# Moving part of a background computation from the first product of a channel mixer to the second one

## The chip, the cores and the metric

The kernel runs on one NeuronCore of a Trainium2 chip. The metric is the device time of one execution in microseconds, as the median of several runs. All work is float32 in and out.

## The reference

Two layers act on a sequence of 1024 tokens with 1024 features. Each layer has a token mixer (layer 0: attention with forget gates, layer 1: gated linear attention) and a channel mixer. Each of the two stands behind an RMS norm whose result is scaled and shifted, and its output is multiplied by a gate. Shift, scale and gate come from a conditioning vector `c`:

```
c_act = jax.nn.silu(c)
mod = c_act @ ada_w[i] + ada_b[i]                  # 6 x 1024 per layer
sh1, sc1, g1, sh2, sc2, g2 = jnp.split(mod, 6)
x = x + g1 * mixer_i(modulate(rms_norm(x, norm1_g[i]), sh1, sc1))
h = modulate(rms_norm(x, norm2_g[i]), sh2, sc2)
x = x + g2 * ((silu(h @ gate) * (h @ up)) @ ffn_w_out[i])   # hidden size 2816
```

The six vectors of a layer do not depend on `x`, so the kernel computes them one at a time beside other work. The second layer's vectors are numbered from 0 here; the "second modulation vector" is `sc1` of layer 1 (the pair `(1, 1)` in the code). It is first needed when layer 1 norms its input, right after the channel mixer of layer 0.

## The kernel before

**Products.** Every float32 operand is split into a rounded part `hi` and a rest `lo`, and `mm3` (lines 317, 318, 319) issues three matmuls for each 128x128 block of weights: hi by hi, hi by lo, lo by hi. ScalarE makes `hi` (line 175), VectorE the rest (line 176). Line 319 is the one that needs the `lo` of the weights. The same lines 175 and 176 serve every such split.

**The channel mixer** is the function `ffn`. Its first product (`h @ ffn_w_in`) goes through 22 groups, a gate group and an up group for each of 11 pairs of hidden tiles. Two groups are computed plainly (`plain_tile`); the other 20 stand in the loop `for X in gs[2:]`. Each of these does seven block products in place of eight, by sums of operands. One block product is a call of `prod`, with 4 blocks, so 12 matmuls into one PSUM bank. VectorE adds the banks up (line 1745), ScalarE and GpSimd form the gated hidden tiles (lines 1728, 1730), GpSimd forms sums of them (lines 1703 to 1713), and they are stored to DRAM (line 1675). GpSimd also forms the sums of weights (lines 978 to 996).

The second product (`... @ ffn_w_out`) runs over three chunks of the hidden tiles, with 3, 4 and 4 tile pairs. Chunks 0 and 1 are the loop `for c_ in range(OC - 1)`: four blocks `i`, each with seven calls of `prod`, of 9 matmuls in chunk 0 and 12 in chunk 1. VectorE adds the results onto tiles `x` and `z` (line 1956). At the end of each block of chunk 1, GpSimd combines them (lines 1970 to 1974), and VectorE adds the gated result to the residual (line 1977), which was loaded from `x_sp` (line 1889). In the last of the four blocks the additions of line 1977 are put off. The third chunk accumulates in PSUM banks `f0a`, `f0b` and so on, and line 2005 adds them. Its operands `B11o`, `T1o`, `T2o`, `B22o` are fetched by line 1860 during chunk 1, and those named `ex_s` there are raw and are split on chip into `T3o` (line 1622 on ScalarE, line 1623 on VectorE). The third chunk's first group reads `B11o`, then `T1o`, then `T2o`.

**The modulation vectors** run beside this. `Pace` is a queue of generators with a balance: each call adds its argument to the balance, and as long as the balance is not negative the next step of a generator is emitted and its price is taken off. `prod` calls two such queues. `ada1` (line 1739) does gate 2 of layer 0 and vector 0 of layer 1 into `ad_s` (lines 541, 543). `ada1l` (line 1740) does the second vector of layer 1 with `ada_one`: it loads 256 KB of `ada_w` in four DMAs into the single buffer `far` (line 454), and two VectorE operations (line 497 for the very first, line 499 otherwise) multiply it and add it to `near`, 16 times over. One such round of a load and two operations is called a step here. Its price is 2.0: 0.5 behind the operations and 1.5 behind the next load. The next load overwrites `far`, so it waits on the two operations. After the 16th step the generator yields 500.0, so its closing product (`ada_end`, line 460, four small matmuls on `near`) is made only by the flush behind chunk 1.

**What sets the order.** The kernel gives no hand-written order for these engines. A scheduler of the tile framework places each engine's instructions, from the order in which they are emitted, their dependencies and its own estimates; `tc.issue_after(last_of("D"))` makes each operation of line 499 come behind the VectorE instruction emitted last before it. Each engine then works in its fixed order, and so does the SyncE queue that issues all these DMAs: an instruction that waits holds what stands behind it.

Of the kernel before, what the change touches and what calls it, by code (L numbers as in the profile page):

```python
# [53 lines left out]
def trunk(ctx, tc, x, c, ada_w, ada_b, norm1_g, norm2_g, ffn_w_in, ffn_w_out,  # L54
# [513 lines left out]
            while self.q:  # L568
                self(1.0)

    late_rate = [0.03]
    ada0, ada0p, ada1, ada1l = Pace(), Pace(), Pace(), Pace()

    def ada1_queue(js, acc, raws_):
# [1004 lines left out]
    def ffn(l, oh, xs, slots, nm, mid, norm_end, each=None, blocks=None):  # L1579
# [142 lines left out]
        def dest(G, key):  # L1722
            return tmpv[TMP[key]] if G.kind else gate_view(G.i, key)

        def fin(G, key):
            d = gate_view(G.i, key)
            if G.kind == 0:
                nc.scalar.activation(d, d, AF.Silu)
                return
            nc.gpsimd.tensor_mul(d, d, dest(G, key))  # L1730
            hid_done(G.i, key)

        def prod(w, t):
            ps = pin([P, HALF], F32, f"p{l}")
            n = len(t)
            for k in range(n):
                mm3(ps, w.hi[:, k, :], w.lo[:, k, :], hi(t[k]), lo(t[k]), k == 0, k == n - 1)
            tick()
            ada1(0.64 * n)
            ada1l(late_rate[0] * n)  # L1740
            return ps

        def add(G, key, ps, src=None):
            d = dest(G, key)
            nc.vector.tensor_add(d, d if src is None else dest(G, src), ps)  # L1745
# [101 lines left out]
        def part(c_):  # L1847

            raw_ = late_raw if c_ else early_raw
            n_k = ODS[c_]  # L1850
            nms = ONAMES if c_ < OC - 1 else ENAMES
            order = list(range(7 * n_k)) if c_ else list(FIRST)
            tiles, ys = o[c_], {}
            for nm_ in ONAMES:
                tiles[nm_] = [None] * n_k
            at = lambda n: (nms[n // n_k], n % n_k)

            def fetch(dst, src):
                with tc.issue_after(pre[0]) if pre else ExitStack():
                    nc.sync.dma_start(dst, src)  # L1860
                if c_ == OC - 1:
                    pre[:] = [last_of("S")]

            def load_raw(n):
                nm_, k = at(n)
                if is_raw(nm_, OAT[c_] + k) and n not in ys:
                    ys[n] = raw_()
                    fetch(ys[n], hid_d[(nm_, OAT[c_] + k)])

            pre = []  # L1870
            for j, n in enumerate(order):
                nm_, k = at(n)
                t = tiles[nm_][k] = big.tile([P, 2, HALF], FR, tag=SL[c_][n], name=f"{nm_}o{l}{c_}{k}")
                load_raw(n)
                if n in ys:
                    split_t(t, ys[n])
                else:
                    fetch(t.bitcast(F32), hid_d[(nm_, OAT[c_] + k)])
                for ahead in order[j + 1:j + 4]:
                    load_raw(ahead)  # L1880
                yield
# [11 lines left out]
        def advance(n):  # L1893
            while n_nxt[0] < n:
                next(nxt[0], None)
                n_nxt[0] += 1

        for X in gs[2:]:
            up = lambda n: advance(n) if X is gs[-1] else None
            if X is gs[-2]:  # L1900
                ada1.flush()
                late_rate[0] = 0.12
                nxt[0] = part(0)
                advance(4)
            nc.scalar.copy(dest(X, C11), prod(feed.next(), B11))
            p5 = prod(feed.next(), T1)
            up(8)
            add(X, C12, prod(feed.next(), T2), C11)
            up(11)
            add(X, C11, prod(feed.next(), B21))  # L1910
            fin(X, C11)
            add(X, C22, prod(feed.next(), T3), C12)
            add(X, C12, p5)
            up(15)
            add(X, C21, prod(feed.next(), T4), C22)
            fin(X, C21)
            add(X, C22, p5)
            fin(X, C22)
            up(20)
            add(X, C12, prod(feed.next(), B22))  # L1920
            fin(X, C12)
            up(21)
# [163 lines left out]

    ADA_A, ADA_B = 6.0, 3.0
    ffn(0, oh, xs, slots, "fo", lambda: mid(5, 6), norm_mixer)
    h1 = hs1
    after_norm = marks.pop("G0")  # L2090
# [525 lines left out]

    ADA_A, ADA_B = 12.0, 6.0
    ffn(1, None, xs, slots, "go", lambda: mid(11), final_norm, final_scale, (out_blocks, out_ends))
    dump("xb1", xs)

# [28 lines left out]
```

## Time and profile before

| | |
|---|---|
| median of 3 runs | 2345.26 us (2344.12 to 2349.59) |
| the profiled execution's own time | 2345.56 us |
| its span, first to last instruction | 2343.8 us |
| busy: TensorE / VectorE / ScalarE / GpSimd | 2322.6 / 1772.7 / 1128.0 / 1160.5 us |
| mean granted clock of TensorE | 0.997 |
| moved by DMA | 390.72 MB |

Times inside the profile are microseconds from the start of the span. The loop of the first product with its 20 groups lies at about 683 to 1068, chunk 0 of the second product at 1068 to 1125, chunk 1 at 1125 to 1201, and the third chunk starts at 1201.7. Layer 1 follows. In the views, PE is TensorE, DVE is VectorE, ACT is ScalarE, POOL is GpSimd and SP is SyncE, whose queue issues the DMAs. A bracket behind an instruction gives the idle time of its engine before it and what ended it. The profile models the ends of matmuls, so PE's busy time overstates how well it is used; the starts of matmuls show its pace.

### The profile page before, as it was taken

The page shows a single profiled execution, that of the slowest core. Times are in us where ns is not written, and L with a number is a line of the kernel's source. Part 1 is how long each engine was busy: PE and PEld are TensorE (multiplying, and loading weights), DVE is VectorE, ACT ScalarE, POOL GpSimd, SP SyncE. Part 2 cuts the span into 40 slices and gives each one's busy share as a digit, 9 for nine tenths or more (in the row PEclk, how much of TensorE's full clock was granted, in tenths as well). Part 3 has the DMA queues.
Part 4 walks back from the last instruction along what each step waited for, and adds up shares of the span by engine and source line. Part 5 has one row for each costly group of instructions (what it writes and reads, how often), then busy time and mean ns, then how long its engine had stood idle before and what let it go on. Part 6 is the DMA issues. An engine that isn't in the chain of part 4 may idle for free.

```text
span 2343.8 us, 35552 instructions
## 1 busy us (share of the span) xinstructions
PE 2322.6 (99%) x12088; PEld 1980.6 (85%) x12088; DVE 1772.7 (76%) x2946; ACT 1128.0 (48%) x2166; POOL 1160.5 (50%) x1027
## 2 busy tenths in 40 slices
PE   8999999999999999999999999999999999999999
PEld 7988888888888888788888899898888888888888
DVE  6577677776788888997888666668787777876787
ACT  6566566675544333334325654345444333345236
POOL 1345454533446656665563522345456666664651
PEclk9999999999999999999999999999999999999999
DMA  8533343352435545459774443555434544458674
GB/s 259 163 99 112 109 120 107 113 169 84 153 100 175 187 158 176 154 203 315 267 265 155 136 128 99 151 171 172 150 102 162 174 147 159 141 189 300 237 264 141
DMA packets 359342, 390.72 MB, mean 167 GB/s; under 512 B 26908, under 2 KB 296376, under 8 KB 359160
## 3 DMA queue, kind: packets, MB, share of 16 engines
q1 hardware_dynamic: 359160, 388.45, 50.7%
q8 instruction: 95, 1.56, 0.3%
q14 instruction: 87, 0.71, 0.1%
HBM read 287.10 MB, written 101.25 MB: 166 GB/s over the span
## 4 chain that ended last, share of the span: by engine, by line
PE 54%; DVE 4%; DMA 3%; POOL 2%; issue 2%; SPq 0%; ACT 0%; POOLq 0%; DVEq 0%; ACTq 0%
PE p_b L317 11%; PE p_b L319 11%; PE p_b L318 11%; PE gv_b L317 1%; PE gv_b L319 1%; PE gv_b L318 1%; PE gr_b L317 1%; PE gr_b L319 1%; PE gr_b L318 1%; DVE o_s L176 1%; DVE ad_s L543 1%; DMA ex_s<-x_sp 1%; PE gqp_b L317 0%; PE gk_b L317 0%; PE f1a_b L319 0%
## 5 line engine op out<-in xcount | busy, mean ns | idle before, releaser
L175 ACT CAST o_s<-xv_s 128x512 fp32r<-128x512 f32 (+1 forms) x392 | 235.9, 610 | 328.4 <-PE p_b L319 218.5
L176 DVE TENSOR_TENSOR o_s<-xv_s,o_s 128x512 fp32r<-128x512 f32 (+1 forms) x392 | 332.7, 854 | 37.2 <-ACT o_s L175 36.3
L317 PE MATMUL p_b<-B,o_s 128*128 128x512 f32 x608 | 235.4, 391 | 0.9 <-DVE ex_s L1745 0.5
L318 PE MATMUL p_b<-B,o_s 128*128 128x512 f32 x608 | 236.1, 389 | 0.0
L319 PE MATMUL p_b<-B,o_s 128*128 128x512 f32 x608 | 235.1, 389 | 0.0
L978 POOL TENSOR_TENSOR ex_s<-xv_s,xv_s 128x512 f32<-128x512 f32 (+1 forms) x64 | 96.0, 1499 | 238.8 <-DMA xv_s<-in_ffn_w_in_dram 123.3
L1362 POOL TENSOR_SCALAR lp_s<-lp_s,st 128x128 f32<-128x128 f32 (+7 forms) x128 | 98.9, 775 | 220.9 <-DVE st L1361 191.8
L317 PE MATMUL p_b<-T,o_s 128*128 128x512 f32 x480 | 186.7, 390 | 1.8 <-DVE x L1745 1.8
L318 PE MATMUL p_b<-T,o_s 128*128 128x512 f32 x480 | 186.7, 389 | 0.0
L319 PE MATMUL p_b<-T,o_s 128*128 128x512 f32 x480 | 181.2, 389 | 0.0
L1360 ACT ACTIVATE lp_s<-lp_s,st 128x128 f32<-128x128 f32 (+7 forms) x128 | 99.5, 777 | 85.4 <-DVE st L1356 68.1
L317 PEld LDWEIGHTS p_b<-B,o_s 128*128 128x128 f32 x608 | 114.1, 188 | 26.6 <-issue 1.6
L319 PEld LDWEIGHTS p_b<-B,o_s 128*128 128x128 f32 x608 | 114.1, 188 | 23.9
L318 PEld LDWEIGHTS p_b<-B,o_s 128*128 128x128 f32 x608 | 114.2, 188 | 23.2
L980 POOL TENSOR_TENSOR xv_s<-ex_s,xv_s 128x512 f32<-128x512 f32 (+1 forms) x64 | 95.7, 1495 | 51.2 <-DVE o_s L176 47.9
L1745 DVE TENSOR_TENSOR ex_s<-ex_s,p_b 128x512 f32<-128x512 f32 x140 | 94.2, 680 | 29.9 <-PE p_b L319 29.6
L990 POOL TENSOR_TENSOR xv_s<-xv_s,xv_s 128x512 f32<-128x512 f32 x48 | 65.8, 1370 | 97.9 <-issue 54.7
L176 DVE TENSOR_TENSOR pt_s<-t_b,pt_s 128x512 fp32r<-128x512 f32 (+1 forms) x160 | 98.4, 632 | 20.3 <-ACT pt_s L175 19.1
L317 PEld LDWEIGHTS p_b<-T,o_s 128*128 128x128 f32 x480 | 90.1, 188 | 21.3 <-DVE x L1745 2.2
L175 ACT CAST pt_s<-t_b 128x512 fp32r<-128x512 f32 (+1 forms) x160 | 82.6, 544 | 51.1 <-PE t_b L1382 32.6
L319 PEld LDWEIGHTS p_b<-T,o_s 128*128 128x128 f32 x480 | 90.1, 188 | 18.7
L318 PEld LDWEIGHTS p_b<-T,o_s 128*128 128x128 f32 x480 | 90.1, 188 | 18.6
(1539 smaller groups left out, 7378.2 us busy)
## 6 DMA issues: line engine op xcount, KB each, us to landing
xv_s<-in_ffn_w_in_dram SPq DMA_DIRECT2D x176, 256.0 KB, 3.2
hid_B<-x SPq DMA_DIRECT2D x66, 512.0 KB, 3.0
ad_s<-in_ada_w_dram SPq DMA_DIRECT2D x384, 64.0 KB, 2.4
hid_T<-x SPq DMA_DIRECT2D x44, 512.0 KB, 2.9
xv_s<-in_ffn_w_out_dram SPq DMA_DIRECT2D x88, 256.0 KB, 3.6
T2o<-hid_T SPq DMA_DIRECT2D x22, 512.0 KB, 7.0
T1o<-hid_T SPq DMA_DIRECT2D x22, 512.0 KB, 6.2
B11o<-hid_B SPq DMA_DIRECT2D x22, 512.0 KB, 5.9
```

The source lines that it names most:

```text
L175: nc.scalar.copy(hi, src)
L176: nc.vector.tensor_sub(lo, src, hi.bitcast(F32))
L317: nc.tensor.matmul(ps, ah, bh, start=start, stop=False, skip_group_check=chain)
L318: nc.tensor.matmul(ps, ah, bl, start=False, stop=False, skip_group_check=chain)
L319: nc.tensor.matmul(ps, al, bh, start=False, stop=stop, skip_group_check=chain)
L543: nc.vector.scalar_tensor_tensor(acc, raw[:, t], c42[:, o:o + 1], acc, op0=ALU.mult, op1=ALU.add)
L978: nc.gpsimd.tensor_add(s1, a21, a22)
L980: nc.gpsimd.tensor_sub(a11, s1, a11)
L990: nc.gpsimd.tensor_sub(r[A12], r[A12], r[A11])
L1360: nc.scalar.activation(lp, lp, AF.Exp, bias=mcur, scale=-1.0, accum_out=st[:, qi, 2:3])
L1362: nc.gpsimd.tensor_scalar(lp, lp, st[:, qi, 3:4], 1.0, op0=ALU.mult, op1=ALU.mult)
L1745: nc.vector.tensor_add(d, d if src is None else dest(G, src), ps)
```

## The change

Two numbers change, no line is added.

```
@@ -568,7 +568,7 @@
-    late_rate = [0.03]
+    late_rate = [0.0]
...
@@ -1899,7 +1899,7 @@
             if X is gs[-2]:
                 ada1.flush()
-                late_rate[0] = 0.12
+                late_rate[0] = 0.17
```

`late_rate` is what line 1740 adds to the balance of `ada1l` for each block of a product. Before, the first 18 groups of the loop (126 calls with 4 blocks) add 126 x 4 x 0.03 = 15.1, which pays for seven steps; the last two groups and the chunks pay for the rest at 0.12 per block. After, the first 18 groups pay for nothing but the first load; the last two groups give 14 x 4 x 0.17 = 9.5, chunk 0 gives 28 x 3 x 0.17 = 14.3, and the remaining quarter of the 31.5 that the 16 steps need before the last operations comes out of chunk 1. The scheduler places the operations later than they are paid for. Neither the amount of work nor the closing product's place behind chunk 1 changes, and `ada1` keeps its rate. The first step still uses line 497.

VectorE's order in the first product, where the 13th of the 20 groups ends, before; `near` is the step's accumulator, `p_b_91` to `p_b_95` are PSUM banks of block products, `o008s` and `o_s` are weights being split:

```order
L543 SCALAR_TENSOR_TENSOR ad_s_7746<-ad_s_7746,c_165 128x256
L176 TENSOR_TENSOR o008s_s_108_9900<-ex_s_7228,o008s_s_108_9900 128x512
L499 SCALAR_TENSOR_TENSOR near<-far,c_165,near 128x256 x2
L1745 TENSOR_TENSOR x_0_6138<-x_0_6138,p_b_91_9804 128x512
L1745 TENSOR_TENSOR ex_s_7228<-ex_s_7228,p_b_95_9880 128x512
```

The same place after:

```order
L543 SCALAR_TENSOR_TENSOR ad_s_7746<-ad_s_7746,c_165 128x256 x2
L1745 TENSOR_TENSOR x_0_6138<-x_0_6138,p_b_91_9774 128x512
L1745 TENSOR_TENSOR ex_s_7229<-ex_s_7228,p_b_94_9833 128x512
L176 TENSOR_TENSOR o_s_105_9810<-xv_s_7232,o_s_105_9810 128x512
L176 TENSOR_TENSOR o008s_s_108_9870<-ex_s_7228,o008s_s_108_9870 128x512
L1745 TENSOR_TENSOR ex_s_7228<-ex_s_7228,p_b_95_9850 128x512
```

The two operations on `near` are gone from here, and the addition that empties `p_b_91` stands ahead of the split of `o008s` instead of behind it.

VectorE's order in chunk 1, third block, before (`x_4`, `x_5` and `z` are the tiles that the block adds onto):

```order
L176 TENSOR_TENSOR o_s_198_11838<-xv_s_7232,o_s_198_11838 128x512
L1956 TENSOR_TENSOR x_5_6143<-x_5_6143,p_b_45_11820 128x512
L176 TENSOR_TENSOR o033s_s_199_11859<-ex_s_7228,o033s_s_199_11859 128x512
L1956 TENSOR_TENSOR x_4_6142<-x_4_6142,p_b_46_11841 128x512
L1956 TENSOR_TENSOR x_5_6143<-x_5_6143,p_b_46_11841 128x512
L176 TENSOR_TENSOR o_s_200_11878<-xv_s_7232,o_s_200_11878 128x512
L1956 TENSOR_TENSOR x_4_6142<-x_4_6142,p_b_47_11864 128x512
```

The same place after:

```order
L499 SCALAR_TENSOR_TENSOR near<-far,c_165,near 128x256
L1956 TENSOR_TENSOR z_10912<-z_10912,p_b_44_11803 128x512
L499 SCALAR_TENSOR_TENSOR near<-far,c_165,near 128x256
L176 TENSOR_TENSOR o_s_198_11838<-xv_s_7232,o_s_198_11838 128x512
L1956 TENSOR_TENSOR x_5_6143<-x_5_6143,p_b_45_11820 128x512
L176 TENSOR_TENSOR o033s_s_199_11859<-ex_s_7228,o033s_s_199_11859 128x512
L499 SCALAR_TENSOR_TENSOR near<-far,c_165,near 128x256
L1956 TENSOR_TENSOR x_4_6142<-x_4_6142,p_b_46_11841 128x512
L1956 TENSOR_TENSOR x_5_6143<-x_5_6143,p_b_46_11841 128x512
L499 SCALAR_TENSOR_TENSOR near<-far,c_165,near 128x256
L176 TENSOR_TENSOR o_s_200_11878<-xv_s_7232,o_s_200_11878 128x512
L1956 TENSOR_TENSOR x_4_6142<-x_4_6142,p_b_47_11864 128x512
```

Two steps stand here where there was none, and a third one follows behind `p_b_48`. Over chunk 1, the four blocks now hold 1, 3, 3 and 0 steps; before they held none.

The queue of SP at the end of that third block, before (`x_sp` is the residual, `xv_s` weights, `T1o` an operand of the third chunk):

```order
L1860 DMA B11o_11895<-hid_B_7388 128x1024
L960 DMA xv_s_7231<-in_ffn_w_out_dram 128x4x128
L1889 DMA ex_s_7230<-x_sp_7309 128x512
L1889 DMA ex_s_7229<-x_sp_7309 128x512
L960 DMA xv_s_7232<-in_ffn_w_out_dram 128x4x128 x2
L960 DMA xv_s_7233<-in_ffn_w_out_dram 128x4x128
L1860 DMA T1o_11959<-hid_T_7370 128x1024
```

The same place after:

```order
L960 DMA xv_s_7231<-in_ffn_w_out_dram 128x4x128
L1860 DMA B11o_11895<-hid_B_7388 128x1024
L1889 DMA ex_s_7230<-x_sp_7309 128x512
L1889 DMA ex_s_7229<-x_sp_7309 128x512
L454 DMA far<-in_ada_w_dram 32x2x256 x8
L960 DMA xv_s_7232<-in_ffn_w_out_dram 128x4x128 x2
L960 DMA xv_s_7233<-in_ffn_w_out_dram 128x4x128
L1860 DMA T1o_11959<-hid_T_7370 128x1024
```

The loads of two steps, eight DMAs, now stand ahead of three loads of weights and of `T1o`.

More of the change, by code (lines that the diff above doesn't have):

```diff
@@ L569, in flush @@
                 self(1.0)
-    late_rate = [0.03]
+    late_rate = [0.0]
     ada0, ada0p, ada1, ada1l = Pace(), Pace(), Pace(), Pace()
@@ L1901, in ffn @@
                 ada1.flush()
-                late_rate[0] = 0.12
+                late_rate[0] = 0.17
                 nxt[0] = part(0)
```

## Prediction

> **What bounds the kernel now.** I read the page first, then the waits of PE from 640 to 1260, then the busy times by stretches, then the timelines of the two places where the change acts.
>
> ```profile
> span 2343.8 us, 35552 instructions
> PE 2322.6 (99%) x12088; PEld 1980.6 (85%) x12088; DVE 1772.7 (76%) x2946; ACT 1128.0 (48%) x2166; POOL 1160.5 (50%) x1027
> ```
>
> PE's list of work bounds the kernel: it is idle 21.2 us of 2343.8. A change that leaves the matmuls alone can only take away or add waits of PE. Those of the channel mixer of layer 0 that the waits view names:
>
> ```profile
> PE p_b L317 <- DVE x L1745: 1.8, 1, 1.8
> PE f0a_b L319 <- DVE o_s L176: 0.8, 1, 0.8
> PE p_b L317 <- DVE ex_s L1745: 0.5, 1, 0.5
> ```
>
> All three are waits for VectorE. By stretches (PE, PEld, DVE, ACT, POOL, each busy us and instructions, then clock, DMA share and GB/s): first product, chunk 0, blocks 2 and 3 of chunk 1, start of the third chunk.
>
> ```profile
> 700.00:1030.00 330.00, 327.37 (x1441) 268.65 (x1440) 284.68 (x362) 124.83 (x214) 200.36 (x134) 1.00 0.53 171
> 1068.00:1125.00 57.00, 57.00 (x253) 47.18 (x253) 40.76 (x58) 30.29 (x61) 30.31 (x23) 1.00 0.92 307
> 1144.00:1163.00 19.00, 19.00 (x85) 15.74 (x84) 14.83 (x19) 4.26 (x7) 13.75 (x9) 1.00 0.55 167
> 1163.00:1182.00 19.00, 19.00 (x85) 15.75 (x84) 15.40 (x19) 4.25 (x7) 13.14 (x10) 1.00 0.42 138
> 1201.30:1214.00 12.70, 11.80 (x52) 9.00 (x51) 8.80 (x16) 1.82 (x4) 6.70 (x7) 1.00 1.06 382
> ```
>
> Chunk 0 shows PE at its full pace, 252 starts in 57.00 us, 4.42 per us. At that pace the first row would hold 1459 + 1; it holds 1441. 19 matmuls of 0.226 us are 4.3 us lost there: 2.63 as idle time, the rest as slow first matmuls behind a wait. The last row would hold 57; it lacks 5, so about 1.1 us. What the change can win at most is 4.3 + 1.1 = 5.4 us, 0.23% of 2345.56. A measurement of this kernel can tell about 0.3%, or 7.0 us, from no change.
>
> **First product: seven steps leave.** A step is two operations on `near` and four loads into `far`.
>
> ```profile
> L499 DVE SCALAR_TENSOR_TENSOR near<-far,c,near x31: 469/485/1512, 715.0 to 1125.2; 128x256 f32<-128x256 f32 x31
> 943.92 1.23 DVE L176 TENSOR_TENSOR o008s_s<-ex_s,o008s_s 128x512 fp32r<-128x512 f32 x1 [2.30 <-ACT o008s_s L175]
> 945.08 2.02 DVE L499 SCALAR_TENSOR_TENSOR near<-far,c,near 128x256 f32<-128x256 f32 x2
> 947.02 0.68 DVE L1745 TENSOR_TENSOR x<-x,p_b 128x512 f32<-128x512 f32 x1
> 945.61 0.39 PE L318 MATMUL p_b<-T,o_s 128*128 128x512 f32 x1
> 947.75 0.50 PE L317 MATMUL p_b<-T,o_s 128*128 128x512 f32 x1 [1.76 <-DVE x L1745]
> 944.68 1.61 POOL L980 TENSOR_TENSOR xv_s<-ex_s,xv_s 128x512 f32<-128x512 f32 x1
> ```
>
> The longest wait of the stretch hangs on one step: its pair holds VectorE from 945.08 to 947.02, the addition that frees PE's bank comes behind it, and PE starts 947.75 instead of 945.84, 1.9 us late. After the change the pair is gone, and the addition is placed ahead of the split of `o008s` that itself waited 2.30 for ScalarE. It can then run before 943.9, and this wait goes whole: -1.9. Of the other 2.4 us I take 0.2, since other steps stand within microseconds of shorter waits. What is late next there is the other queue's operations (line 543), which stay. So -2.1, between 0 (the new order puts another operation in the way) and -4.3.
>
> The pair took 1.94, not twice 0.48, because its first operation ran beside POOL's of 944.68 (1.5 of the longest 1.512).
> [...]
> [...]
>
> The 28 loads that leave relieve SP's queue by 28 issues, but weights waited for VectorE, not for SP; I take 0.
>
> **Chunk 1: seven steps arrive,** 1, 3, 3, 0 by blocks. PE doesn't wait in chunk 1 (19.00 of 19.00), so what VectorE hands to it there comes early enough, and I take a delay of VectorE of a few us, about the 2.7 of one product of 12 matmuls, to cost PE nothing at once. It costs at the start of the third chunk, through POOL and SP. The third block and what follows:
>
> ```profile
> 1124.74 0.99 DVE L499 SCALAR_TENSOR_TENSOR near<-far,c,near 128x256 f32<-128x256 f32 x2
> 1125.64 1.29 DVE L176 TENSOR_TENSOR o_s<-xv_s,o_s 128x512 fp32r<-128x512 f32 x2
> ...
> 1173.57 1.40 DVE L176 TENSOR_TENSOR o_s<-xv_s,o_s 128x512 fp32r<-128x512 f32 x1
> 1174.90 0.67 DVE L1956 TENSOR_TENSOR x<-x,p_b 128x512 f32<-128x512 f32 x1
> 1175.49 1.18 DVE L176 TENSOR_TENSOR o033s_s<-ex_s,o033s_s 128x512 fp32r<-128x512 f32 x1
> 1176.60 1.27 DVE L1956 TENSOR_TENSOR x<-x,p_b 128x512 f32<-128x512 f32 x2
> 1178.52 1.23 DVE L176 TENSOR_TENSOR o_s<-xv_s,o_s 128x512 fp32r<-128x512 f32 x1 [0.64 <-ACT o_s L175]
> 1179.67 0.68 DVE L1956 TENSOR_TENSOR x<-x,p_b 128x512 f32<-128x512 f32 x1
> 1180.27 1.19 DVE L176 TENSOR_TENSOR o_s<-xv_s,o_s 128x512 fp32r<-128x512 f32 x1
> 1182.64 0.75 DVE L1977 SCALAR_TENSOR_TENSOR x<-x,modc,ex_s 128x512 f32<-128x512 f32 x1 [1.18 <-POOL x L1970]
> 1185.77 1.88 DVE L1977 SCALAR_TENSOR_TENSOR x<-x,modc,ex_s 128x512 f32<-128x512 f32 x1 [1.18 <-POOL x L1972]
> 1190.03 1.41 DVE L1977 SCALAR_TENSOR_TENSOR x<-x,modc,ex_s 128x512 f32<-128x512 f32 x2 [1.19 <-POOL x L1974]
> 1180.87 1.74 POOL L1970 TENSOR_TENSOR x<-x,z 128x512 f32<-128x512 f32 x1
> 1185.81 1.29 POOL L1973 TENSOR_TENSOR x<-x,z 128x512 f32<-128x512 f32 x1
> 1171.22 0.98 SPq L1889 DMA_DIRECT2D ex_s<-x_sp  x2
> 1179.81 5.17 SPq L960 DMA_DIRECT2D xv_s<-in_ffn_w_out_dram  x3
> 1187.13 2.36 SPq L1860 DMA_DIRECT2D T1o<-hid_T  x4
> 1206.06 0.62 ACT L1622 CAST T3o<-ex_s 128x512 fp32r<-128x512 f32 x1 [6.09 <-DMA ex_s<-hid_T]
> 1208.07 0.68 DVE L176 TENSOR_TENSOR o_s<-xv_s,o_s 128x512 fp32r<-128x512 f32 x1
> 1208.80 0.51 PE L319 MATMUL f0a_b<-B11o,o_s 128*128 128x512 f32 x1 [0.82 <-DVE o_s L176]
> L454 SPq DMA_DIRECT2D far<-in_ada_w_dram x64: 560/585/1009, 579.0 to 1117.6; - x64
> DMA to landing us min/median/max: 2.2/3.1/7.7
> ```
>
> This is one chain. The operands of the third chunk may be fetched from when POOL is done with the third block's line 1973 (1185.81 + 1.29 = 1187.10; `T1o` is issued 1187.13). SP then issues a dozen large DMAs one behind the other, the raw operand among them reaches ScalarE at 1206.06, the split of the weights stands behind it, and PE waits for that until 1208.80. It has no slack: what POOL is late at 1187, PE is late at 1208.
>
> Undisturbed, a pair adds 1125.64 - 1124.74 = 0.90 to VectorE. A block holds waits of 0.64 + 1.18 + 1.18 + 1.19 = 4.2 us, so three pairs (2.7) fit if they stand in them. In blocks 1 and 2, with 1 and 3 steps, one pair stands right ahead of line 1977, and additions for the next block move into POOL's waits; I take 0 left over. In block 3 the first pair (+0.90) moves the split of `o033s` to 1176.4 to 1177.6. The second pair needs data whose loads cannot be issued before the first pair is done. That one stands a split (1.33 from start to start) and an addition (0.59) ahead of `o033s`, so it is done at 1176.4 - 1.9 = 1174.5. Three issues of 0.585 later, at 1176.3, the fourth load starts, and it lands 2.2 to 3.1 later, at 1178.5 to 1179.4. VectorE waits 0.9 to 1.8 for it, and behind it wait the additions of `p_b_46` and all of the block. They start 1179.8 at the later end, 3.2 late; the 0.64 for ScalarE is then absorbed and the second half of the pair added, which leaves the addition of `p_b_47` 3.0 late, ending at 1183.3 in place of 1180.3. POOL's line 1970 had 0.5 to spare, so it starts 1183.4, 2.5 late. The third pair stands in the wait for line 1972 and costs 0. `T1o` is issued 1189.6. SP's loads of weights behind the eight loads of `far` slip from 1179.81 to about 1184 and land before line 978 needs them; DMA has room there (0.42). So PE's wait grows by 2.5. Its bounds are 0 (all in the waits) and +6.6: four operations of blocks 2 and 3 beside POOL's, 1.51 each instead of 0.48, add 4.1.
>
> The closing product needs the last pair, which runs near 1188, against 1201: 0.
>
> **Sum,** against the profiled execution's own 2345.56, which is 0.30 above the median of the runs shown: 2345.56 - 2.1 + 2.5 = 2345.96. I predict 2346.0.
>
> **Rivals.** *A. The waits of chunk 1 take up all seven steps.* For it: 4.2 us of waits in each block. Against it: the loads of the second pair in block 3 can't be early. 2345.56 - 2.1 = 2343.5.
>
> *B. Slower: VectorE's pairs and POOL shut each other out in chunk 1.* If all six operations of a block run at 1.51 they take 9.1 us, 4.9 more than the block's 4.2 of waits; two such blocks put line 1973 and with it the third chunk 9.8 late: 2345.56 - 2.1 + 9.8 = 2353.3, +0.33%. It decides once `T1o` is issued more than 9.1 us later against PE than now. For it: POOL busy 70%. Against it: the median of 31 operations is 485 ns.
> [...]
>
> *C. The new order of the first product brings a wait like the one that goes.* The scheduler's estimates are not the chip's, and VectorE's rows moved all along the stretch: with two such waits of 1.9 on top of the forecast, 2346.0 + 3.8 = 2349.8. For it: the old order had one. Against it: VectorE has 14 operations less.
>
> *D. All waits of both stretches go:* 2345.56 - 5.4 = 2340.2, still within 0.3%. Faster by more would need waits that this profile doesn't have. The change does what it says; the order shows it.
>
> **Numbers.** Forecast 0.55, A 0.23, C 0.08 and D 0.02 lie within 0.3%: same 0.88. B has 0.10. Faster keeps 0.02 for runs that differ by more than their own spread. The range reaches from the lower bound of the first term with A, 2345.56 - 4.3 = 2341.3, to the forecast with the contended 4.1 and one uncovered pair of 0.9, 2351.0; B and some of D stay outside.
>
> **What would show it.** Right: no line 499 between 700 and 1030, PE busy there above 329 of 330, no wait of 1.8 at line 1745; line 499 in chunk 1 with a wait for `far` of 1 to 2 us before the additions of `p_b_46`; `T1o` issued about 2.5 later against the end of chunk 1; a wait of about 3.3 in place of 0.82 for `o_s` in `f0a`. Wrong: PE waiting inside chunk 1, a new wait over 1 us in the first product, or a third chunk that starts without a longer wait.

## The result and the profile after

The changed kernel takes 2356.21 us, the median of 6 runs (2353.87 to 2358.88); the kernel before takes 2345.74 (6 runs, 2344.12 to 2349.59). The ratio is 1.0042, with a 95% interval of 1.0031 to 1.0053. That is 10.5 us slower, outside the range on record, and nearest to the time of rival B (2353.3).

The head of the page of the changed kernel:

```profile
span 2354.7 us, 35543 instructions
PE 2326.6 (99%) x12088; PEld 1983.0 (84%) x12088; DVE 1766.6 (75%) x2946; ACT 1125.4 (48%) x2166; POOL 1157.8 (49%) x1027
```

What TensorE waits for between 640 and 1260 us (total, times, longest):

```profile
PE f0a_b L317 <- ACT o_s L175: 4.5, 1, 4.5
PE f0a_b L319 <- DVE o_s L176: 1.4, 1, 1.4
PE p_b L317 <- DMA B22o<-hid_B: 1.4, 2, 1.1
PE p_b L319 <- DVE o_s L176: 1.3, 5, 0.4
PE p_b L317 <- DVE ex_s L1745: 0.8, 1, 0.8
PE p_b L319 <- DVE o033ss_s L176: 0.8, 1, 0.8
```

The wait of 1.8 for `x` of line 1745 is gone, as predicted. Six other waits are new or have grown, and their places tell the story. The same by stretches, with the columns of the prediction: first product, chunk 0, blocks 1 to 3 of chunk 1 (by the clock of before), block 4, start of the third chunk:

```profile
700.00:1030.00 330.00, 329.96 (x1459) 273.16 (x1458) 272.97 (x354) 126.70 (x219) 205.08 (x138) 1.00 0.51 169
1065.00:1125.00 60.00, 58.37 (x254) 47.08 (x253) 43.80 (x59) 30.35 (x61) 29.82 (x23) 1.00 0.90 291
1125.00:1144.00 19.00, 17.60 (x77) 13.74 (x76) 14.66 (x22) 6.93 (x14) 6.13 (x5) 1.00 1.06 346
1144.00:1163.00 19.00, 18.88 (x84) 15.30 (x83) 15.46 (x20) 4.02 (x7) 13.13 (x10) 1.00 0.88 283
1163.00:1182.00 19.00, 19.00 (x85) 15.75 (x84) 17.15 (x23) 3.14 (x6) 11.70 (x8) 1.00 0.49 150
1182.00:1205.30 23.30, 21.96 (x95) 16.93 (x93) 19.35 (x26) 4.05 (x7) 13.00 (x9) 1.00 0.57 194
1205.30:1222.00 16.70, 10.78 (x37) 8.01 (x37) 14.41 (x21) 3.52 (x6) 12.99 (x10) 0.80 1.01 372
```

Blocks 1 and 4 before:

```profile
1125.00:1144.00 19.00, 19.00 (x86) 15.73 (x85) 15.17 (x22) 6.54 (x11) 9.50 (x6) 1.00 1.05 381
1182.00:1201.30 19.30, 19.30 (x86) 15.97 (x86) 15.65 (x20) 4.26 (x7) 13.44 (x10) 1.00 0.73 261
```

The first product holds 1459 matmuls in 330 us, all that fit, where before held 1441. Behind it, chunk 0 and blocks 1 and 4 of chunk 1 lose time (block 1 holds 77 matmuls in place of 86), and the third chunk's start holds 37 matmuls in 16.70 us, where 74 would fit. Blocks 2 and 3 lose next to nothing on TensorE.

For a comparison of all runs I use two measures, both taken from the records of each trace. The *loss* of a stretch is the sum of what a matmul starts later than 0.227 us behind the one before it, over all spacings above 0.300. The part of the program ahead of the first product, which no kernel here changes, ends anywhere from 630.6 to 635.6 us in these profiles, so single spans can't be compared to better than that. The *issue of T1o* is the start of line 1860's first `T1o` load for the third chunk, counted from the first matmul on a `p_b` bank (635.23 in before, 635.33 in after), so that this drops out.

```
kernel    loss in us: first product, chunk 0, chunk 1, third chunk = sum    T1o
before                4.59          0.00     0.00     2.02         6.61   551.90
after                 0.50          2.69     4.90     8.89        16.98   561.25
change               -4.1          +2.7     +4.9     +6.9        +10.4    +9.35
```

So the first product gave 4.1, and three later stretches took 14.5. Three places of the trace of after show how.

**Chunk 0.** The vector now begins from nothing at the end of the first product, just when line 1860 fetches the operands of chunk 0. SP's issues, VectorE and TensorE there:

```profile
1048.46 1.03 SPq L1860 DMA_DIRECT2D B11o<-hid_B  x2
1049.59 3.08 SPq L454 DMA_DIRECT2D far<-in_ada_w_dram  x4
...
1058.03 0.49 DVE L499 SCALAR_TENSOR_TENSOR near<-far,c,near 128x256 f32<-128x256 f32 x1 [3.17 <-DMA far<-in_ada_w_dram]
1058.43 0.69 DVE L1745 TENSOR_TENSOR ex_s<-ex_s,p_b 128x512 f32<-128x512 f32 x1
...
1066.85 0.47 PE L317 MATMUL p_b<-T3o,o_s 128*128 128x512 f32 x1 [0.84 <-DVE ex_s L1745]
```

The load of `far` is queued between 512 KB loads of operands. VectorE, whose list is in order, stands 3.17 us in front of an operation of 0.49, and the additions to `ex_s` that free TensorE's banks stand behind it. From there to TensorE's wait VectorE has no idle time. This wait makes 1.1 of chunk 0's 2.69. The other 1.6 come at 1086.29, 1088.86 and 1099.56, where TensorE waits for VectorE's splits of weights (line 176). In the chain view, late loads of weights lie ahead of them (`xv_s`, 5.64 and 7.54 us).

That the load stands among operands doesn't explain it by itself. The kernel before has such loads there too, and loses nothing in chunk 0:

```profile
1045.62 1.88 SPq L454 DMA_DIRECT2D far<-in_ada_w_dram  x3
1056.76 2.63 SPq L454 DMA_DIRECT2D far<-in_ada_w_dram  x4
```

**Blocks 2 and 3 of chunk 1.** VectorE's steps (two pairs of block 2, both beside GpSimd, and an operation of block 3), then GpSimd and SP up to the issue of `T1o`:

```profile
1164.41 2.03 DVE L499 SCALAR_TENSOR_TENSOR near<-far,c,near 128x256 f32<-128x256 f32 x2
...
1170.76 2.88 DVE L499 SCALAR_TENSOR_TENSOR near<-far,c,near 128x256 f32<-128x256 f32 x2
...
1185.81 0.48 DVE L499 SCALAR_TENSOR_TENSOR near<-far,c,near 128x256 f32<-128x256 f32 x1 [1.58 <-DMA far<-in_ada_w_dram]
...
1172.00 1.35 POOL L1973 TENSOR_TENSOR x<-x,z 128x512 f32<-128x512 f32 x1
...
1194.94 1.61 POOL L1973 TENSOR_TENSOR x<-x,z 128x512 f32<-128x512 f32 x1
...
1180.56 9.88 SPq L454 DMA_DIRECT2D far<-in_ada_w_dram  x8
1190.53 5.28 SPq L960 DMA_DIRECT2D xv_s<-in_ffn_w_out_dram  x3
1196.59 1.76 SPq L1860 DMA_DIRECT2D T1o<-hid_T  x4
```

The wait for `far` of 1.58 is the one that the prediction placed there (0.9 to 1.8). `T1o` is again issued when line 1973 of the third block ends (1196.55). But that end is late: from the second block's (1172.00 + 1.35 = 1173.35) to the third's it is 23.2 us, and 21.0 from the first's to the second's; before, it was 19.6 from block to block. Its rows for blocks 1 and 2 before (block 3 stands in the prediction):

```profile
1146.61 1.30 POOL L1973 TENSOR_TENSOR x<-x,z 128x512 f32<-128x512 f32 x1
1166.22 1.29 POOL L1973 TENSOR_TENSOR x<-x,z 128x512 f32<-128x512 f32 x1
```

**The start of the third chunk.** TensorE:

```profile
1215.52 0.80 PE L317 MATMUL f0a_b<-B11o,o_s 128*128 128x512 f32 x1 [4.48 <-ACT o_s L175]
1216.11 0.63 PE L318 MATMUL f0a_b<-B11o,o_s 128*128 128x512 f32 x1
1218.17 0.80 PE L319 MATMUL f0a_b<-B11o,o_s 128*128 128x512 f32 x1 [1.44 <-DVE o_s L176]
1218.77 0.63 PE L317 MATMUL f0a_b<-B11o,o_s 128*128 128x512 f32 x1
1219.20 0.63 PE L318 MATMUL f0a_b<-B11o,o_s 128*128 128x512 f32 x1
```

Two waits of 5.9 us together, where there was 0.82; and behind them matmuls that start 0.43 apart, not 0.227, until 1222. The granted clock is 0.80 over the whole window of 1205.30 to 1222.00. Eight such spacings (1.6 us) and two of 0.59 (0.7 us) are 2.3 us that no wait shows.

### The profile page after: what moved, and what is told of

The parts are those of the page before. It is cut to its first block, busy times and chain, and to the rows that moved or that the text cites. A ratio compares the mean times of both kernels' runs of the same rounds, so it can differ in the third digit from the quotient of the medians.

```text
span 2354.7 us, 35543 instructions
## 1 busy us (share of the span) xinstructions
PE 2326.6 (99%) x12088; PEld 1983.0 (84%) x12088; DVE 1766.6 (75%) x2946; ACT 1125.4 (48%) x2166; POOL 1157.8 (49%) x1027
## 4 chain that ended last, share of the span: by engine, by line
PE 69%; DMA 4%; DVE 3%; POOL 2%; issue 1%; SPq 0%; ACT 0%; POOLq 0%; DVEq 0%; ACTq 0%
PE p_b L319 14%; PE p_b L317 14%; PE p_b L318 14%; PE gv_b L317 1%; PE gv_b L319 1%; PE gv_b L318 1%; PE gr_b L317 1%; PE gr_b L319 1%; PE gr_b L318 1%; DMA xv_s<-in_ffn_w_out_dram 1%; DMA T2o<-hid_T 1%; PE o_b L1396 1%; PE t_b L1382 1%; DMA B21o<-hid_B 1%; DVE o_s L176 0%
```

## The experiments

Theory L, formed on these traces: the seven steps in chunk 1 delay the chain of VectorE, GpSimd and SP that ends in `T1o`, and the third chunk with it. Its rivals: the new order of matmuls and weights costs, not the steps (O); only VectorE's operations cost (D); only the loads and SP's issues cost (S, later T for the transfer time).

### The seven steps of chunk 1, whole and in halves

e1 leaves them out, e2 keeps their loads and shortens their operations, e3 keeps the operations and leaves the loads out. Each edit is to `ada_one` of the changed kernel:

```diff
 e1
-        for n in range(16):
+        for n in range(9):
...
-            if n < 15:
+            if n < 8:
 e2, in line 499, w_ = slice(0, 256 if n < 9 else 8)
-                        nc.vector.scalar_tensor_tensor(acc, raw[:, t], c42[:, o:o + 1], acc,
+                        nc.vector.scalar_tensor_tensor(acc[:, w_], raw[:, t, w_], c42[:, o:o + 1], acc[:, w_],
 e3
-                ada_load(raw, l, j, n + 1, 2)
+                n < 8 and ada_load(raw, l, j, n + 1, 2)
```

> The changed kernel with the seven steps that it puts into chunk 1 left out altogether, both VectorE operations and the loads of far (so the second modulation vector lacks seven sixteenths of its sum). The order of the matmuls stays that of the changed kernel up to chunk 1 and differs in one matmul in it. Theory L: the loss is the lag that these seven steps give to VectorE, POOL and SP in chunk 1; waits in chunk 1 go (about 5 us) and the start of the third chunk comes back (about 8 us), so 2343 to 2345, and below the kernel before by the first product's 4 us less the 2.6 us that chunk 0 lost. Rival O: the loss is the changed order of matmuls and weights around the steps, not the steps; then the waits of chunk 1 and the 4.5 us wait of the third chunk stay and it reads 2350 or more.

> The changed kernel with the two VectorE operations of each of the seven steps of chunk 1 cut from 256 columns to 8 (most of these seven rows of the sum are left out); all loads of far stay, and so does the order of the matmuls and of SP's queue. Theory D: what costs is the time of the operations on VectorE, longer beside POOL; then within 2 us of the run without the steps, 2343 to 2347. Rival S: what costs is the 28 loads, on SP's queue ahead of B22o, the weights and T1o, and VectorE's waits for them; then 2352 to 2356, with the wait for far in block 3 still there and T1o still 8 us or more late.

> The changed kernel with the loads of far for the seven steps of chunk 1 left out (their operations work on the rows that are in far already, so the second modulation vector is another). Free of the loads, the operations are placed earlier: one step more in chunk 0, three in block 1 and two in block 2 of chunk 1, and one between. Theory D: the operations cost wherever they stand in chunk 1; 2349 to 2355, with VectorE's rows of block 3 late and T1o late by 5 us or more. Rival S: loads cost, so this reads like the run without the steps, 2343 to 2346.

Measured:

```
kernel        us       ratio to before, 95%         loss: first, c0, c1, third = sum      T1o
e1 neither    2348.68  1.0010 [1.0001, 1.0019]      0.50  3.26  0.00  5.49 =  9.25   553.70
e2 loads      2355.28  1.0035 [1.0022, 1.0048]      0.52  2.51  3.00  9.27 = 15.30   559.55
e3 operations 2352.44  1.0029 [1.0017, 1.0040]      0.50  2.94  0.96  9.18 = 13.58   557.93
```

Rival O falls: without the seven steps the waits of chunk 1 are gone, with the order of matmuls as good as unchanged. But e1 stays above the 2343 to 2345 that theory L gave: chunk 0 keeps its 3.3, and the third chunk still loses 5.5. D and S fall both, each by the run that was to show it alone: either half of the steps brings back half of the loss or more. In terms of `T1o`, the seven steps are worth 561.25 - 553.70 = 7.55 us; with loads alone it is 5.85, with operations alone 4.2. The operations of e3 stand earlier, none of them in block 3, so e3 doesn't price them in the places that they have in the changed kernel.

Why the halves don't add up is seen in e2, where an operation has 8 columns. VectorE's rows of blocks 2 and 3, and GpSimd beside the first of them:

```profile
1166.38 2.46 DVE L499 SCALAR_TENSOR_TENSOR near<-far,c,near 128x8 f32<-128x8 f32 x2
...
1173.81 0.22 DVE L499 SCALAR_TENSOR_TENSOR near<-far,c,near 128x8 f32<-128x8 f32 x1
...
1181.14 0.49 DVE L499 SCALAR_TENSOR_TENSOR near<-far,c,near 128x8 f32<-128x8 f32 x2 [2.88 <-DMA far<-in_ada_w_dram]
...
1186.08 0.23 DVE L499 SCALAR_TENSOR_TENSOR near<-far,c,near 128x8 f32<-128x8 f32 x1 [2.06 <-DMA far<-in_ada_w_dram]
...
1165.84 1.61 POOL L1972 TENSOR_TENSOR x<-x 128x512 f32<-128x512 f32 x1 [1.53 <-DVE x L1956]
1167.53 1.29 POOL L1973 TENSOR_TENSOR x<-x,z 128x512 f32<-128x512 f32 x1
```

Alone, such an operation takes 0.22. Beside GpSimd a pair of them takes 2.46 here: the first ends as line 1972 ends (1167.45), the second as line 1973 does (1168.82). The length of the operation hardly matters here, its turn does. And the waits for `far`, 2.88 and 2.06, are there with 8 columns too.

### Each edit by itself

```diff
 e4, from the kernel before
-                late_rate[0] = 0.12
+                late_rate[0] = 0.17
 e6, from the kernel before
-    late_rate = [0.03]
+    late_rate = [0.0]
```

> Only the second of the two edits: pace 0.03 until the last two groups as before, then 0.17 in place of 0.12. The number of operations in each stage stays that of the kernel before, and so does the order of the matmuls; only places within chunk 0 differ. Theory L: the higher pace alone costs nothing, 2345.7 within 1 us. Rival: the chunk 0 that the changed kernel shows with 2.6 us of new waits comes from the higher pace; then 2348 or more.

> Only the first of the two edits: pace 0 until the last two groups, then 0.12 as before. Fewer steps are done early: 3 in the last two groups, 5 in chunk 0, then 1, 3, 1, 2 by blocks of chunk 1 and one behind it. Theory L (the lag at the end of block 3 sets the third chunk): block 3 has one step in place of three, so T1o is 2 to 4 us less late than in the changed kernel, 2351 to 2354. Rival: the loss goes with the number of steps behind chunk 0, eight in place of seven; then as the changed kernel or worse, 2355 to 2358.

```
e4 pace only      2344.69  0.9997 [0.9988, 1.0006]   4.18  0.00  0.00  2.50 =  6.69   552.24
e6 late start     2352.00  1.0019 [1.0010, 1.0028]   0.70  3.19  2.39  8.62 = 14.90   558.88
```

The higher pace alone does nothing that can be measured. The late start alone is slower and loses the same 3 us in chunk 0. With one step in the third block in place of three, `T1o` comes 2.4 earlier than in the changed kernel, as theory L said.

### No vector at all

```diff
 e5, from the changed kernel, with a memset of the sum
-        ada_load(raw, l, j, 0, 2)
...
-        for n in range(16):
+        for n in range(1):
```

> The changed kernel without the second modulation vector of the second layer: all 16 steps, their operations and their loads, are left out (a memset stands for the sum). Theory F, that the steps feed every loss, those of chunk 0 too: first product without waits as in the changed kernel, chunk 0 and chunk 1 without waits, third chunk 2 us or less as before, so 2346 - 4.1 = 2342 or below. Rival P: PE, 4 us earlier out of the first product, runs into what SP, DMA and POOL deliver anyway, steps or none; then chunk 0 keeps 2 to 3 us of waits, the third chunk 4 to 5 us, and it reads 2345 to 2348.

2339.74 us, ratio 0.9964 [0.9951, 0.9977]: loss 1.04, 0, 0, 0, with `T1o` at 546.57. Between 640 and 1260 TensorE has one wait:

```profile
PE p_b L317 <- DVE x L1745: 0.4, 1, 0.4
```

Theory F holds, P falls: the waits of chunk 0 come with the steps. It also prices the whole vector: some 8 us in the kernel before, the most that a better place could save.

### Other places for the steps

e7 and e8 start the vector earlier in the first product; e11 and e14 keep it away from the stretches in which DMA is full (shares of 0.90, 1.06 and 1.01 in the rows of after).

```diff
 e7 (e8: gs[-6] and 0.12), from the changed kernel
+            if X is gs[-4]: late_rate[0] = 0.17
             if X is gs[-2]:
                 ada1.flush()
-                late_rate[0] = 0.17
 e11, from the changed kernel: 0.05 at line 571, 0.0 at line 1902, and in the loop over i
+                late_rate[0] = 0.3 if c_ == 0 and i >= 2 else 0.0
 e14, from the kernel before: 0.0 at line 1902, and in the loop over i
+                late_rate[0] = 0.2 if c_ == 0 and i >= 2 else 0.4 if c_ == 1 and i == 3 else 0.0
```

> As the changed kernel, but the pace of 0.17 starts four groups from the end of the first product, not two. About 8 steps in the first product, 6 in chunk 0, 2 in chunk 1 (1, 1, 0, 0 by blocks). Theory L: chunk 1's part of the loss is nearly gone, so the third chunk is as in the run without the seven steps, and chunk 0 keeps 2 to 3 us: 2347 to 2350. Rival: any step in the last groups of the first product and in chunk 0 costs as much as one in chunk 1; then 2353 or more.

> The vector starts six groups from the end of the first product at 0.12 and stays at 0.12: about 10 steps in the first product, 5 in chunk 0, one in chunk 1 (block 1 of its four). Theory L: the start of the vector, with VectorE's first wait for far, lies in the middle of the first product where DMA has room, so chunk 0 keeps no wait and the third chunk starts as in the kernel before; with at most 2 us of waits in the first product that is 2342 to 2346. Rival P: chunk 0 and the third chunk wait whenever PE leaves the first product early; then 2347 to 2350.

> Both moved on purpose to where DMA has room: pace 0.05 until the last two groups, 0 from there to the middle of chunk 0, then 0.3 in the second half of chunk 0. 12 steps in the first product, 4 in chunk 0, none in chunk 1. Theory T: no waits in chunk 0, the third chunk loses 0 to 2 us (2.0 in the kernel before), the first product 4 to 6 us in place of 4.6, so 2343 to 2347, the kernel before or up to 2 us below it. Rival: the steps cost what they cost wherever they stand; then 2348 or more.

> From the kernel before: pace 0.03 as there until the last two groups, none from there to the middle of chunk 0 and in the first three blocks of chunk 1 (one pair slips into its first), 0.2 in the second half of chunk 0, 0.4 in the fourth block of chunk 1, whose steps T1o doesn't wait for; the flush at its end issues the last two. Theory S: T1o is issued 2 to 4 us earlier than in the kernel before, and TensorE loses at the third chunk 0 to 1 in place of 2.0; 2343 to 2345.5 unless the last steps, now at the start of the third chunk, delay its splits by as much (then 2346 to 2349). Rival, the number of steps behind the first product counts: slower than before by 3 us or more.

```
e7    2357.48  1.0046 [1.0032, 1.0059]   5.94  4.14  3.43  5.22 = 18.72   563.76
e8    2348.15  1.0005 [0.9996, 1.0013]   2.37  0.68  2.32  5.54 = 10.91   555.76
e11   2358.93  1.0053 [1.0040, 1.0066]  21.08  0.00  0.00  1.30 = 22.39   567.49
e14   2349.10  1.0006 [0.9996, 1.0015]   3.93  0.00  0.00  3.52 =  7.45   549.79
```

e7 was a miss for theory L in its first form: only two steps stand in chunk 1 (by the count that gives the changed kernel seven), and it is as slow as the changed kernel. Half the vector is pressed into the last four groups, where VectorE now waits 21.6 us for `far`, in nine waits (4.4 us in three before, 9.6 in seven after). e8, with the start two groups further up and a lower pace, is within 0.3% of the kernel before, but a miss for theory L as well: `T1o` comes 3.9 later than before and the third chunk loses 5.5, and the time lies in the range of rival P (2347 to 2350). e11 was a miss too: in the first product a pace of 0.05 costs 21 us where 0.03 costs 4.6. In e14 `T1o` comes 2.1 earlier than before, as expected, but the last steps now run at the start of the third chunk, which loses 3.5 in place of 2.0, and nothing is won. No version here that keeps the whole vector beats the kernel before by what a measurement can tell.

### Sizes, for the whole vector

e9 cuts the loads behind the first to 8 columns, e10 the operations behind the first row.

```diff
 e9
-                ada_load(raw, l, j, n + 1, 2)
+                ada_load(raw, l, j, n + 1, 2, 8)
 e10
-                        nc.vector.scalar_tensor_tensor(acc, raw[:, t], c42[:, o:o + 1], acc,
+                        nc.vector.scalar_tensor_tensor(acc[:, :8], raw[:, t, :8], c42[:, o:o + 1], acc[:, :8],
```

> The changed kernel with all loads of far behind the first step's cut from 256 columns to 8 (so most of the vector's sum is of stale data); SP issues as many DMAs in the same places, VectorE's operations keep their length. Theory T (transfers: the loads take DMA time in the three stretches in which DMA is full, ahead of chunk 0, of chunk 1 and of the third chunk, and VectorE, POOL and SP wait in turn): most of the loss goes, chunk 0 loses under 1 us, the third chunk under 4, 2341 to 2346. Rival D (the operations on VectorE, and SP's 64 issues): 2350 to 2356 as in the changed kernel.

> The changed kernel with all operations of the vector behind its first row cut from 256 columns to 8 (the sum is left out for the others); all loads stay whole. Theory T: transfers cost, so nearly the whole loss stays, 2350 to 2356, with 2 to 3 us of waits in chunk 0 and 8 to 9 at the third chunk. Rival D: the time of the operations costs; then 2341 to 2346.

```
e9    2355.14  1.0034 [1.0022, 1.0047]   0.52  0.87  4.82  8.16 = 14.37   558.81
e10   2352.26  1.0024 [1.0014, 1.0034]   0.50  1.11  1.85  9.42 = 12.88   556.53
```

Theory T, that the transfer time costs, falls with e9: with 2 KB in place of 64 KB per load, most of the loss stays. The number of packets is the same, but in the DMA records those of `far` took 9 ns in the median in place of 46. The loads of `far` in e9, with the time from issue to landing, and what VectorE waits for them in sum:

```profile
L454 SPq DMA_DIRECT2D far<-in_ada_w_dram x60: 560/567/639, 1040.1 to 1168.8; - x60
...
  DMA far<-in_ada_w_dram: 17.9, 9
...
DMA to landing us min/median/max: 1.9/4.7/8.3
```

A small load lands as late as a large one (3.9 in the median in the changed kernel, 8.4 at most), so its own size isn't what takes the time. That it waits behind the operands in the queue is likely, but no run takes them away. Rival D falls with e10 in the same way. Chunk 0 alone gains in both (0.87 and 1.11 in place of 2.69). Of the 4.82 that e9 loses in chunk 1, 1.6 are matmuls that start 0.40 to 0.43 apart behind a wait of 2.26 for VectorE.

### Does TensorE's lead reach T1o?

In 15 of the 17 kernels, `T1o` less the sum of the losses is between 543.5 and 545.6 (545.3 before, 544.3 after); e14 has 542.3, and e13, with 5.4 us of added work ahead of it that is no loss, 548.7. So the lost time goes with the issue of `T1o`. This alone doesn't say which sets which, since a loss ahead of `T1o` can delay both. In the expectations from e12 on, and in that of e14, "theory S" is that the issue of `T1o` sets the end; it is not the rival S of the halves. e12 and e13 put more work on TensorE, e15 takes steps out of the first product and puts them nowhere.

```diff
 e12 and e13, in prod of the changed kernel, for two products each of layer 0
-            for k in range(n):
+            for k in [*range(n)] * (1 + twice[0]):
 e12
+                    twice[0] = l == 0 and c_ == 1 and i == 3 and j in (1, 3)
 e13
+            twice[0] = l == 0 and X in (gs[-6], gs[-5])
 e15, in ada_one of the kernel before
-                for t in range(2):
+                for t in range(2 if n >= 6 else 0):
...
-                ada_load(raw, l, j, n + 1, 2)
+                n >= 5 and ada_load(raw, l, j, n + 1, 2)
```

> The changed kernel with 24 matmuls more in layer 0: two products of the fourth block of chunk 1 are computed twice, with the same result (24 x 0.227 = 5.4 us of TensorE). Theory S, the issue of T1o sets the end and TensorE waits for it: the wait at the start of the third chunk shrinks by what TensorE now does, and the time stays, 2355 to 2358. Rival W, TensorE's work and waits add up: +5.4, 2361 to 2362.5.

> The changed kernel with 24 matmuls more late in layer 0's first product: one product each of the sixth and fifth group from its end is computed twice, with the same result (5.4 us of TensorE, about what the first product of the kernel before waits). Theory S in its strong form, the loads into chunk 0 and the steps set T1o whenever TensorE comes: T1o moves by less than 2 us and the time by as little, 2355 to 2358. Rival W: chunk 0 starts 5.4 later, and so does everything, 2361 to 2362.5. Between them: T1o moves by a part.

> The kernel before with the first six steps of the vector left out, operations and loads (the ones in the first product ahead of its last groups); the other ten stay at the kernel before's pace, five around the end of the first product and five in chunk 0, none in chunk 1. The first product's 4 us of waits should go. Theory B, what costs is where the vector begins and runs (from scratch into the transfers ahead of chunk 0): here the vector also begins there, so chunk 0 loses 2 to 3 us and T1o comes 1 to 3 us later than in the kernel before: 2346 to 2349. Rival A, the lead in the first product is worth its 4 us when nothing is put into chunk 1: 2341.5 to 2343.

```
e12   2362.63  1.0055 [1.0037, 1.0073]   1.16  2.08  2.07 12.81 = 18.12   562.31
e13   2360.78  1.0058 [1.0044, 1.0072]   0.51  3.29  4.45  9.97 = 18.21   566.89
e15   2345.01  0.9990 [0.9980, 1.0000]   2.27  0.11  0.00  7.00 =  9.38   552.91
```

e12 came out at rival W's time (2361 to 2362.5), not at theory S's 2355 to 2358. `T1o` hardly moves (+1.1), yet TensorE's wait for it doesn't shrink: the two waits at the start of the third chunk grow from 4.5 and 1.4 to 5.0 and 4.0. VectorE's list differs there: two additions of line 1956 and a wait for GpSimd now stand between its split of the raw operand and that of the weights, which are 5.6 us apart in place of 2.5. So the end is not set by the issue of `T1o` alone. What the added matmuls would cost without that delay e12 doesn't show. e13 speaks against the strong form of theory S: 5.4 us more of TensorE late in the first product move `T1o` by 5.6. e15 shows the other side. With six steps simply gone, TensorE reaches chunk 1 2.4 us earlier in the profiled execution (488.5 in place of 490.8 on the scale of `T1o`), yet `T1o` comes 1.0 later, and the third chunk takes the lead back. The 2 to 3 us that theory B expected chunk 0 to lose are not there (0.11):

```profile
PE f0a_b L317 <- ACT o_s L175: 2.0, 1, 2.0
PE f0a_b L319 <- DVE o_s L176: 1.8, 1, 1.8
PE p_b L317 <- DVE sg_s L1745: 1.5, 1, 1.5
```

By the medians (2345.01 against 2347.08) a gain of 2.1 us is left, with an interval from none to 4.7; that is between the two expectations and excludes neither. So a delay of TensorE passed on to `T1o` whole, and how much of this lead counts is open between nothing and all; the profile shows none of it. A lead can pass on whole: in e5, without any step, TensorE reaches chunk 1 4.3 earlier than in the kernel before (486.55 in place of 490.84), and `T1o` comes 5.3 earlier.

## Why the prediction was wrong

**First product, -2.1.** The mechanism was right: the pair went, the wait behind it went, and no new one came (rival C falls). The size was off: "Of the other 2.4 us I take 0.2" should have been nearly all of it, -4.1, the lower end.

**That this gain counts at the end.** Here the sum itself was unsafe. It added what TensorE wins in one stage to what it loses in another. But the prediction had itself found that the third chunk starts by the issue of `T1o`, without slack; a lead of TensorE then counts only if `T1o` comes earlier too. In e1, which has no step behind the start of chunk 1, TensorE reaches chunk 1 0.8 earlier than before and `T1o` comes 1.8 later. e15 takes six steps out and puts them nowhere: 2.1 us by the medians, and none in its profile. In e5 the lead came through, so the term isn't shown to be nothing in every case.

**Chunk 0, not charged.** It holds about as many steps as before (five in place of six), so I looked at no wait there. It lost 2.7 us, and 2.5 to 3.3 in the runs e1, e2, e3 and e6, none with the higher pace alone (e4) and none without the vector (e5). So the late start brings it. How it does is not settled: the kernel before has loads of `far` among the operands too, and e15, whose first operation runs at about 1000 us in place of 1040, loses 0.11.

**"I take 0 left over" in blocks 1 and 2.** This is the step that failed worst. The ends of line 1973, on the scale of `T1o`:

```
                               block 1   block 2   block 3
before                          512.68    532.28    551.87
e1, without the seven steps     515.69    534.07    553.67
after                           517.07    538.02    561.23
```

Against e1 the seven steps make line 1973 late by 1.4, 4.0 and 7.6: blocks 1 and 2 leave 4.0 over, where the prediction had 0. It had fitted pairs of 0.90 into waits of 4.2 by their sum. In the longest measured pair, of 2.88, the operations took 1.45 and 1.39 and ended 0.3 behind lines 1972 and 1973 of GpSimd (1171.93 and 1173.35), so both waited for the instruction beside them; and the next wait in VectorE's list need not stand where it could take that up.

**Block 3.** The wait for `far` came where it was placed, with 1.58 us for 0.9 to 1.8. What the block does to `T1o` was put at +2.5; by the table it adds 3.6, so this term was nearer. By e1 the seven steps together moved `T1o` by 7.55, outside the bound of 6.6 for chunk 1.

**"PE doesn't wait in chunk 1 ... cost PE nothing at once".** It cost 4.90 us. `B22o`, fetched behind loads of `far`, makes TensorE wait 1.4, and VectorE's splits of the weights come late in block 4.

**Rival B** had the right sign and nearly the right time, and that VectorE's pairs wait for GpSimd is shown by the rows of e2 (2.46 for a pair of 8 columns). But it is half of the story: with the loads gone and the operations whole (e3) `T1o` is 4.2 later than in e1, with the operations cut and the loads whole (e2) 5.85. The seven steps cost by two kinds of turn. That its time is near the measured one is partly luck: it put 9.8 on the operations alone and nothing on chunk 0, on TensorE's waits in chunk 1 or on the clock.

**The clock.** The 2.3 us behind the long wait stood in no term. e1, without the seven steps, doesn't have them (its granted clock is 1.00 over 1205.00 to 1222.00).

**What stays open.** Why e1 and e15, with no step in blocks 2 to 4 of chunk 1 and TensorE ahead, issue `T1o` 1.0 to 1.8 later than the kernel before was not settled; e5, without any step, issues it 5.3 earlier. The order of SP's issues ahead of chunk 1 differs there, and GpSimd's line 978 waits for what they fetch; no run took that apart. A second buffer for `far`, which would free a load from the step before it, was not tried.

## What to carry to other kernels

Look for an issue at which the stages join (here a fetch released by GpSimd) and price a move first by how far it moves that issue. A wait that goes upstream of it counts only as far as the issue comes earlier, and e12 and e14 show that the issue isn't all: the splits behind it can cost as much. Leaving a piece of work out altogether tells in one run how much a move could win at most. Here a small background step cost its turn more than its size: an 8-column operation took up to 1.33 us beside GpSimd where a whole one took up to 1.52, and a 2 KB load landed after 4.7 us in the median where a whole one landed after 3.9. So don't move such steps to where TensorE happens not to wait, but to where the engine and the queue that they go through have slack.

## What the runs showed of the hardware that I had not expected

- In e2 an 8-column VectorE operation of line 499 takes 0.22 us alone and up to 1.33 beside a GpSimd addition, ending with it.
- In e9 loads of 2 KB landed 4.7 us after their issue in the median and 8.3 at most while operands were fetched, no sooner than loads of 64 KB in the changed kernel (3.9 and 8.4).
- After the third chunk's waits of 4.48 and 1.44 us matmuls of 512 columns start 427 ns apart for some 3.5 us, and the granted clock is 0.80 over 1205.30 to 1222.00 and 0.50 over 1218.00 to 1222.00. The slow matmuls also came in e15 behind two waits of 2.0 and 1.8 us (0.80 over 1200.00 to 1217.00), and in e9 behind a single one of 2.26 in chunk 1; they didn't come in e1 behind 2.2 and 0.8. What sets them off no run shows.
